# Gate and up projections with 512 moving columns: high and low rows in one matmul, each half in a PSUM bank of its own

## The chip, the cores and the metric

The kernel runs on one core of one Trainium2 chip. The metric is the device time of one execution in microseconds (us). The core has TensorE (PE, with the weight loads shown as PEld), VectorE (DVE), ScalarE (ACT), GpSimd (POOL) and SyncE (SP), which work side by side and wait for one another through semaphores. SBUF is the working memory; PSUM is the memory that TensorE writes into, eight banks of 512 fp32 numbers per partition.

## The reference, cut to what matters

One layer: a mixer (gated MLP beside a gated DeltaNet scan), and then a mixture of 16 experts over 2048 tokens of width 1024. Each expert chooses its 256 tokens, and this part is what the change touches:

```
aff = softmax(h @ w_router + b_router)            # 2048 x 16
gate, idx = top_k(aff of each expert, 256)
xe = h[idx]                                       # 256 x 1024 for each expert
hid = silu(xe @ w_gate[e]) * (xe @ w_up[e])       # 256 x 1024
ye = (hid @ w_down[e]) * gate                     # 256 x 1024
out[idx] += ye
```

All of it is fp32. After the experts comes a last RMSNorm of every token.

## The kernel before, in words

**Products in three parts.** TensorE is given numbers of type fp32r, which keep fewer bits than fp32. So the kernel splits each fp32 operand in two, high (the value cast to fp32r) and low (the value less its high part), and adds three products: high x high, high x low, low x high. `mm3` (L193 to L196) does this for one slice k of 128 of the contraction: L194 is weights high times rows high, L195 weights high times rows low, L196 weights low times rows high, all into the same PSUM columns. A matmul has a stationary operand (128 x 128, loaded ahead of it) and a moving operand, whose columns stream through.

**Loading weights.** `load_w` (L167) brings 512 columns of a weight matrix as two transfers of 256 columns (1 MB each) into `raw`, of which there are two buffers. ACT casts a `raw` into half of the high tile `wh` (L183), DVE subtracts into half of the low tile `wl` (L184). There are three sets of `wh` and `wl`, used in turn (`next_w`). One expert takes six sets, so twelve transfers: gate and up for the first 512 hidden columns, gate and up for the second, and two for down. SyncE issues the transfers in order, each when its buffer is free.

**One expert** (`expert`, L1382). The rows of its tokens come by an indirect gather (`xg`, L1368), are transposed on TensorE into PSUM tiles `xt` (L1376) and split into `xS[0]` (high, by ACT) and `xS[1]` (low, by DVE). The hidden width of 1024 is done in eight pieces f of 128, four for each loaded pair of weights. For each f, one PSUM tile `gu` holds gate in its first 256 columns and up in its second, for the 256 tokens; 8 slices k with 3 matmuls each fill either half, so 48 matmuls of 256 moving columns for one f. Then ACT takes Silu of the gate half (L1396), DVE multiplies with the up half (L1397), ACT casts to the high part of `hS` (L1399) and DVE subtracts for the low part (L1400). The down projection uses `hS` as stationary operand and 512 columns of weights as moving operand, into the tiles `dn`; DVE scales into `ye` (L1416), and POOL adds the rows to `h_rows` by an indirect transfer (L1453). The input of expert e + 1 (`expert_in`: routing with one-hot rows `oh` and matmuls into a tile of pool `c`, then `idx`, gather, transposes) is issued in the middle of expert e. The last three experts add to gathered rows `hr` and write final tokens themselves; during experts 13 and 14 SyncE also loads and stores 16 final tiles of 128 tokens (`final_tile`).

**PSUM in this stage.** Pool `psaD` has three banks for `gu`, `psdD` two for `dn`, `pstD` two for `xt`, and `pscD` one for tile `c`, which serves the top-k search, routing and a few transposes. Eight in all. A `gu` bank comes free when the product (L1397) has read it.

**Order.** Each engine works its own list in order. The lists are made when the kernel is built, by a planner that runs through the program with estimated durations (the tile context is made with `schedule_with_timeline_sim=True`); so matmuls of one expert's down projection stand between those of the next expert's gate and up.

Of the kernel before, what the change touches and what calls it, by code (L numbers as in the profile page):

```python
# [7 lines left out]
F32 = mybir.dt.float32  # L8
F32R = mybir.dt.float32r
# [3 lines left out]
AF = mybir.ActivationFunctionType  # L13
OP = mybir.AluOpType
AX = mybir.AxisListType
PS = bass.MemoryType.PSUM
DR = bass.MemoryType.DRAM

P = 128
D = 1024  # L20
KT = 8
# [1184 lines left out]
def moe(tc, ctx, env):  # L1206
    nc = tc.nc
# [5 lines left out]
    with ExitStack() as pd:  # L1213
# [2 lines left out]
            raw_f = pf.enter_context(tc.tile_pool(name="rawF", bufs=2, side="right"))  # L1216
            pre = [load_w(raw_f, wr, w[0, 0, :, 0:512], nc.gpsimd, parts=PP, cast=C1) for w in (w_gate, w_up)]
        rt = pd.enter_context(tc.tile_pool(name="rtD", bufs=1))
        ps_a = pd.enter_context(tc.tile_pool(name="psaD", bufs=3, space=PS))
        ps_d = pd.enter_context(tc.tile_pool(name="psdD", bufs=2, space=PS))  # L1220
        ps_t = pd.enter_context(tc.tile_pool(name="pstD", bufs=2, space=PS))
        ps_c = pd.enter_context(tc.tile_pool(name="pscD", bufs=1, space=PS))

        tk = ExitStack()
        wk = tk.enter_context(tc.tile_pool(name="wkT", bufs=1))
        vp = ps_c.tile([P, 2, P], F32, name="c")
        for s in range(2):
            nc.tensor.transpose(vp[:, s, :], AFF[:, s].rearrange("p e g -> p (e g)"), ident)
        blkb, belb, cand, step, cK, siob = topc
# [11 lines left out]
        candp = cps[:, 0, 0:60].rearrange("p (i j) -> p i j", j=4)  # L1241
        nc.scalar.activation(candp, cand, AF.Copy)
        for i in range(15):
            tp = ps_c.tile([P, 512], F32, name="c")
            nc.tensor.matmul(tp[:, 0:3], blkb, cK, start=True, stop=False)
            cn = wk.tile([P, 2], BF, name="cn", bufs=15)
            for j in range(2):
                jk = wk.tile([P, 256], BF, name=f"jk{j}", bufs=1)
                cj = nc.vector.tensor_scalar(jk, X, cd[:, j:j + 1], None, op0=OP.is_le, op1=OP.add,
                                             accum_out=cn[:, j:j + 1])  # L1250
            if i == VI:
                after_first = cj
            ca = wk.tile([P, 1], BF, name="ca", bufs=15)
            jk = wk.tile([P, 256], BF, name="jk2", bufs=1)
            with nc.allow_low_precision(reason="whole numbers up to 256 are exact"):
                nc.scalar.activation(jk, X, AF.Sign, scale=-1.0, bias=cd[:, 2:3], accum_out=ca)
            nc.tensor.matmul(tp[:, 0:2], blkb, cn, start=False, stop=False)
            nc.tensor.matmul(tp[:, 2:3], blkb, ca, start=False, stop=True)
            if i not in (6, 14):
                tcd = cps[:, 1, 4 * i:4 * i + 4]  # L1260
                nc.vector.tensor_scalar(tcd, candp[:, i + 1, :], cd[:, 3:4], None, op0=OP.add)
            if i == 14:
                lob = wk.tile([P, 1], F32, name="lob", bufs=1)
                nc.vector.tensor_scalar(lob, cd[:, 3:4], -1.0, float(LO0), op0=OP.mult, op1=OP.add)
            ge = wk.tile([P, 3], F32, name="ge", bufs=15)
            inc = wk.tile([P, 1], F32, name="inc", bufs=15)
            nc.vector.scalar_tensor_tensor(ge, tp[:, 0:3], CAP - 0.5, step[:, i:i + 1].to_broadcast([P, 3]),
                                           op0=OP.is_ge, op1=OP.mult, accum_out=inc)
            if i == 6:
                npre = wk.tile([P, 1], F32, name="npre", bufs=1)  # L1270
                nc.vector.tensor_tensor(npre, cd[:, 3:4], inc, op=OP.subtract)
                t1 = wk.tile([P, 256], U16, name="t1", bufs=1)
                t2 = wk.tile([P, 256], U16, name="t2", bufs=1)
                nc.vector.scalar_tensor_tensor(t1, nhi, npre, nlow, op0=OP.is_equal, op1=OP.mult)
                nc.vector.tensor_scalar(t2, nhi, npre, float(LO0), op0=OP.is_gt, op1=OP.mult)
                nc.vector.tensor_tensor(t1, t1, t2, op=OP.max)
                X = t1
                cd = cand[:, 7, :]
                hb = wk.tile([P, 1], I32, name="hb", bufs=1)
                nc.vector.tensor_scalar(hb, npre, -65536.0, 65536.0 * HI0, op0=OP.mult, op1=OP.add)  # L1280
            elif i < 14:
                cd = wk.tile([P, 4], F32, name="cd", bufs=15)
                nc.vector.tensor_scalar(cd, tcd, inc, None, op0=OP.subtract)
# [7 lines left out]
        eq = wk.tile([P, 256], BF, name="eq", bufs=1)  # L1291
        nc.vector.tensor_scalar(gt, V, thr, None, op0=OP.is_gt, op1=OP.add, accum_out=ct[:, 0:1])
        nc.vector.tensor_scalar(eq, V, thr, None, op0=OP.is_equal, op1=OP.add, accum_out=ct[:, 1:2])
        tp = ps_c.tile([P, 512], F32, name="c")
        nc.tensor.matmul(tp[:, 0:2], belb, ct, start=True, stop=True)
        nc.tensor.matmul(tp[:, 2:3], blkb, ct[:, 0:1], start=True, stop=True)
        off = wk.tile([P, 3], F32, name="off", bufs=1)
# [11 lines left out]
        nc.vector.scalar_tensor_tensor(se, se, off[:, 1:2], eq, op0=OP.add, op1=OP.mult)  # L1309
        nc.vector.scalar_tensor_tensor(sg, sg, BIG, se, op0=OP.add, op1=OP.add)  # L1310
        SL = rt.tile([P, 2, NE, 8], F32, name="SL", bufs=1)
        sp = ps_c.tile([P, 2, P], F32, name="c")
        for s in range(2):
            nc.tensor.transpose(sp[:, s, :], sg[:, s * P:(s + 1) * P], ident)
        nc.vector.tensor_copy(SL.rearrange("p s e g -> p s (e g)"), sp)
# [16 lines left out]
        wk = pd.enter_context(tc.tile_pool(name="wkD", bufs=1))  # L1332

        def route(e):
            oh = ohp.tile([P, 2, 8, 256], BF, name="oh", bufs=1)
            for s in range(2):
                for g in range(8):
                    nc.vector.tensor_scalar(oh[:, s, g, :], siob, SL[:, s, e, g:g + 1], None, op0=OP.is_equal)
            rp = ps_c.tile([P, 2, 256], F32, name="c")
            for hf in range(2):  # L1340
                for i in range(16):
                    s, g = divmod(i, 8)
                    nc.tensor.matmul(rp[:, hf, 0:5], oh[:, s, g, hf * P:(hf + 1) * P], vals[:, s, e, g, :],
                                     start=(i == 0), stop=(i == 15))
            idx = rt.tile([P, 2], I32, name="idx", bufs=2)
            with nc.allow_low_precision(reason="token numbers are whole"):
                nc.vector.tensor_reduce(idx, rp[:, :, 0:2], axis=AX.X, op=OP.add)
            rs = rt.tile([P, 2, 5], F32, name="rs", bufs=2)
            nc.vector.tensor_copy(rs, rp[:, :, 0:5])
            gate = rt.tile([P, 2], F32, name="gate", bufs=2)  # L1350
            nc.vector.tensor_tensor(gate, rs[:, :, 2], rs[:, :, 3], op=OP.add)
            nc.vector.tensor_tensor(gate, gate, rs[:, :, 4], op=OP.add)
            return idx, gate
# [10 lines left out]
        def expert_in(e):  # L1364
            idx, gate = route(e)
            xg = wk.tile([P, 2, D], F32, name="xg", bufs=1)
            for hf in range(2):
                last[1] = nc.gpsimd.indirect_dma_start(out=xg[:, hf, :], out_offset=None, in_=f_rows,  # L1368
                                                       in_offset=bass.IndirectOffsetOnAxis(ap=idx[:, hf:hf + 1], axis=0))
            xS = [wk.tile([P, KT, 256], F32R, name=f"xS{s}", bufs=1) for s in range(2)]  # L1370
            for kk in range(4):
                ps = ps_t.tile([P, 2, 256], F32, name="xt")
                for k2 in range(2):
                    for hf in range(2):
                        k = 2 * kk + k2
                        nc.tensor.transpose(ps[:, k2, hf * P:(hf + 1) * P], xg[:, hf, k * P:(k + 1) * P], ident)  # L1376
                ks = slice(2 * kk, 2 * kk + 2)
                nc.scalar.activation(xS[0][:, ks, :], ps, AF.Copy)
                last[0] = nc.vector.tensor_tensor(xS[1][:, ks, :], ps, xS[0][:, ks, :].bitcast(F32), op=OP.subtract)
            return idx, gate, xS  # L1380

        def expert(e, st, mid=None):  # L1382
            idx, gate, xS = st
            nx = None
            hS = [wk.tile([P, KT, 256], F32R, name=f"hS{s}", bufs=1) for s in range(2)]
            for i in range(2):
                gw = next_w(w_gate[0, e, :, i * 512:(i + 1) * 512])
                uw = next_w(w_up[0, e, :, i * 512:(i + 1) * 512])
                for f in range(4):
                    fs = slice(f * P, (f + 1) * P)  # L1390
                    pg = ps_a.tile([P, 2, 256], F32, name="gu")
                    for j, w in enumerate((gw, uw)):
                        for k in range(KT):
                            mm3(pg[:, j, :], w[0][:, k, fs], w[1][:, k, fs], xS[0][:, k, :], xS[1][:, k, :], k, KT)
                    sg_ = wk.tile([P, 256], F32, name="sgl", bufs=2)
                    nc.scalar.activation(sg_, pg[:, 0, :], AF.Silu)  # L1396
                    nc.vector.tensor_tensor(sg_, sg_, pg[:, 1, :], op=OP.mult)  # L1397
                    ff = 4 * i + f
                    nc.scalar.activation(hS[0][:, ff, :], sg_, AF.Copy)  # L1399
                    nc.vector.tensor_tensor(hS[1][:, ff, :], sg_, hS[0][:, ff, :].bitcast(F32), op=OP.subtract)  # L1400
                if mid is not None and i == 0:
                    nx = mid()
# [192 lines left out]
```

## Time and profile before

| | |
|---|---|
| Time, median of 3 runs (range) | 2490.78 us (2490.44 to 2491.81) |
| Profiled execution: its own time | 2490.03 us |
| Profiled execution: span from first to last instruction | 2488.2 us |
| Mean granted TensorE clock | 0.974 of full speed |
| Busy share of PE, DVE, ACT, POOL | 95%, 64%, 45%, 21% |
| HBM traffic over the span | 211 GB/s |

The page cuts the span into 40 slices and gives each engine's busy share by slice in tenths. A group of instructions (same line, engine, operation and tile) has its busy time, the mean of one in ns, and the idle time of the engine just ahead of it with what ended that. Matmuls are pipelined: one's printed duration overlaps the next one's, so what a matmul costs in a row of them is the time from one start to the next. The chain of waits goes back from the last instruction to what released each step.

### The profile page before, as it was taken

To read this page: it belongs to the slowest core of one execution; us is meant where nothing else is said; L and a number is where in the kernel's file an instruction comes from. 1 tells how busy PE (TensorE), PEld (TensorE's weight loads), DVE (VectorE), ACT (ScalarE), POOL (GpSimd) and SP (SyncE) were. 2 spreads that over 40 slices of the span, in tenths; PEclk is the share of its full clock that TensorE was granted. 3 is DMA by queue.
4 is the path that set the end of the run, shared out by engine and by line. 5 is a ranking of instruction groups with operands and counts; after the bars stand their busy time and mean duration, and the time that the engine had idled before them with its cause. 6 is when DMAs were issued, how large, how long until landed. Compare 5 with 4: busy or idle time off the path is not lost.

```text
span 2488.2 us, 43191 instructions
## 1 busy us (share of the span) xinstructions
PE 2358.8 (95%) x16841; PEld 2156.8 (87%) x16841; DVE 1584.1 (64%) x3339; ACT 1115.6 (45%) x2004; POOL 533.7 (21%) x451
## 2 busy tenths in 40 slices
PE   7999999999997989999949999999999999999998
PEld 4999999887776888888838899999999999998897
DVE  7588765458778646576774556555565565556675
ACT  4554555567633443333332444444444444444453
POOL 2321222211114553232250101101111011011111
PEclk9999999999998999999978999999999999999999
DMA  8676655489956897655563667666676666668884
GB/s 267 199 229 208 208 172 164 134 269 325 284 142 192 253 278 233 197 187 175 174 189 111 203 187 223 199 205 204 203 220 200 207 219 199 210 203 261 305 301 166
DMA packets 473056, 528.97 MB, mean 213 GB/s; under 512 B 104500, under 2 KB 392061, under 8 KB 470803
## 3 DMA queue, kind: packets, MB, share of 16 engines
q1 hardware_dynamic: 455298, 465.63, 58.6%
q0 software_dynamic: 17120, 59.77, 8.3%
q8 instruction: 133, 2.18, 0.4%
q10 hardware_dynamic: 432, 0.79, 0.1%
q14 instruction: 73, 0.59, 0.1%
HBM read 400.45 MB, written 125.67 MB: 211 GB/s over the span
## 4 chain that ended last, share of the span: by engine, by line
PE 45%; DMA 9%; DVE 3%; issue 3%; ACT 1%; POOL 1%; SPq 0%; POOLq 0%; DVEq 0%; ACTq 0%
PE gu L196 7%; PE gu L194 7%; PE gu L195 7%; PE dn L194 4%; PE dn L195 4%; PE dn L196 4%; DMA xg<-f_rows,idx 4%; PE mx L194 2%; PE mx L196 2%; PE mx L195 2%; DMA raw<-in_w_gate_dram 1%; ACT wh L183 1%; PE xt L1376 1%; DVE wl L184 1%; DMA raw<-in_w_up_dram 1%
## 5 line engine op out<-in xcount | busy, mean ns | idle before, releaser
L184 DVE TENSOR_TENSOR wl<-raw,wh 128x2048 fp32r<-128x2048 f32 (+1 forms) x214 | 450.4, 2116 | 294.2 <-ACT wh L183 291.4
L194 PE MATMUL gu<-xS,wh 128*128 128x256 f32 x2048 | 582.8, 286 | 6.6 <-ACT wh L183 4.7
L196 PE MATMUL gu<-xS,wl 128*128 128x256 f32 x2048 | 580.4, 286 | 4.2 <-DVE wl L184 4.2
L195 PE MATMUL gu<-xS,wh 128*128 128x256 f32 x2048 | 582.0, 285 | 0.0
L183 ACT ACTIVATE wh<-raw 128x2048 fp32r<-128x2048 f32 (+1 forms) x218 | 381.8, 1771 | 356.0 <-DMA raw<-in_w_gate_dram 142.7
L194 PEld LDWEIGHTS gu<-xS,wh 128*128 128x128 f32 x2048 | 395.9, 194 | 8.7 <-ACT wh L183 5.3
L196 PEld LDWEIGHTS gu<-xS,wl 128*128 128x128 f32 x2048 | 394.2, 193 | 6.0 <-DVE wl L184 5.0
L195 PEld LDWEIGHTS gu<-xS,wh 128*128 128x128 f32 x2048 | 396.1, 193 | 1.1
L194 PE MATMUL pj<-aS,wh 128*128 128x258 f32 x832 | 238.7, 290 | 3.1 <-DVE y L460 2.7
L195 PE MATMUL pj<-aS,wh 128*128 128x258 f32 x832 | 239.0, 288 | 0.2 <-DVE aS L358 0.2
L196 PE MATMUL pj<-aS,wl 128*128 128x258 f32 x832 | 238.3, 288 | 0.9 <-DVE wl L184 0.9
L1453 POOL DMA_INDIRECT h_rows<-ye,idx x26 | 67.4, 2591 | 659.8 <-DVE ye L1416 565.7
L194 PE MATMUL dn<-wh,hS 128*128 128x512 f32 (+1 forms) x520 | 202.7, 390 | 0.0
L195 PE MATMUL dn<-wl,hS 128*128 128x512 f32 (+1 forms) x520 | 201.2, 387 | 0.0
L196 PE MATMUL dn<-wh,hS 128*128 128x512 f32 (+1 forms) x520 | 200.3, 386 | 0.0
L194 PEld LDWEIGHTS pj<-aS,wh 128*128 128x128 f32 x832 | 157.7, 191 | 4.7 <-issue 2.4
L195 PEld LDWEIGHTS pj<-aS,wh 128*128 128x128 f32 x832 | 159.2, 191 | 0.6 <-DVE aS L358 0.4
L196 PEld LDWEIGHTS pj<-aS,wl 128*128 128x128 f32 x832 | 158.5, 191 | 1.3 <-DVE wl L184 1.1
L194 PE MATMUL uv<-wh,ast 128*128 128x512 f32 x384 | 153.1, 399 | 0.0
L196 PE MATMUL uv<-wh,ast 128*128 128x512 f32 x384 | 150.2, 391 | 0.0
L195 PE MATMUL uv<-wl,ast 128*128 128x512 f32 x384 | 149.8, 390 | 0.0
L1399 ACT ACTIVATE hS<-sgl 128x256 fp32r<-128x256 f32 x128 | 53.1, 415 | 181.9 <-DVE sgl L1397 181.6
(480 smaller groups left out, 4562.7 us busy)
## 6 DMA issues: line engine op xcount, KB each, us to landing
raw<-in_w_gate_dram SPq DMA_DIRECT2D x64, 1024.0 KB
raw<-in_w_up_dram SPq DMA_DIRECT2D x64, 1024.0 KB
raw<-in_w_down_dram SPq DMA_DIRECT2D x64, 1024.0 KB
kv<-kv SPq DMA_DIRECT2D x140, 256.0 KB
raw<-in_w_mod_dram SPq DMA_DIRECT2D x18, 1024.0 KB
a_sp<-aS SPq DMA_DIRECT2D x32, 512.0 KB
ast<-a_sp POOLq DMA_DIRECT2D x16, 1024.0 KB, 8.6
raw<-in_w_in_dram SPq DMA_DIRECT2D x12, 1024.0 KB
```

The lines of the kernel that those rows point to most:

```text
L183: nc.scalar.activation(wh[:, ks, s:s + 256], raw[:, ks], AF.Copy)
L184: (lo_eng or nc.vector).tensor_tensor(wl[:, ks, s:s + 256], raw[:, ks], wh[:, ks, s:s + 256].bitcast(F32), op=OP.subtract)
L194: pace(nc.tensor.matmul(ps, ah, bh, start=(k == 0), stop=False), after)
L195: nc.tensor.matmul(ps, ah, bl, start=False, stop=False)
L196: return nc.tensor.matmul(ps, al, bh, start=False, stop=(k == nk - 1))
L1376: nc.tensor.transpose(ps[:, k2, hf * P:(hf + 1) * P], xg[:, hf, k * P:(k + 1) * P], ident)
L1399: nc.scalar.activation(hS[0][:, ff, :], sg_, AF.Copy)
L1453: nc.gpsimd.indirect_dma_start(out=h_rows, out_offset=bass.IndirectOffsetOnAxis(ap=idx[:, hf:hf + 1], axis=0), in_=ye[:, hf, :], in_offset ...
```

## The change

The two tiles `xS[0]` and `xS[1]` become one tile `xS` with the high and the low rows one after the other. For one k of gate (or up), a single matmul takes weights high as stationary operand and moves both, 256 columns of high rows and 256 of low rows (two stretches of SBUF that lie 8 x 256 numbers apart), into a whole bank: columns 0 to 255 get high x high, 256 to 511 get high x low. A second matmul adds weights low x rows high to the first 256 columns. So gate and up of one f need a bank each; `psaD` has four banks, and `pscD` goes: its tiles now come out of `pstD`, under the name `xt`, in turn with the transposes. When a bank is done, ACT copies its second half to SBUF and DVE adds the first half to it; for gate, ACT then takes Silu in SBUF; when up is done as well, DVE multiplies the two in SBUF.

```diff
-        ps_a = pd.enter_context(tc.tile_pool(name="psaD", bufs=3, space=PS))
+        ps_a = pd.enter_context(tc.tile_pool(name="psaD", bufs=4, space=PS))
         ps_d = pd.enter_context(tc.tile_pool(name="psdD", bufs=2, space=PS))
         ps_t = pd.enter_context(tc.tile_pool(name="pstD", bufs=2, space=PS))
-        ps_c = pd.enter_context(tc.tile_pool(name="pscD", bufs=1, space=PS))
+        ps_c = ps_t
...
-        vp = ps_c.tile([P, 2, P], F32, name="c")
+        vp = ps_c.tile([P, 2, P], F32, name="xt")
...
-            rp = ps_c.tile([P, 2, 256], F32, name="c")
+            rp = ps_c.tile([P, 2, 256], F32, name="xt")
...
-            xS = [wk.tile([P, KT, 256], F32R, name=f"xS{s}", bufs=1) for s in range(2)]
+            xS = wk.tile([P, 2, KT, 256], F32R, name="xS", bufs=1)
...
-                nc.scalar.activation(xS[0][:, ks, :], ps, AF.Copy)
-                last[0] = nc.vector.tensor_tensor(xS[1][:, ks, :], ps, xS[0][:, ks, :].bitcast(F32), op=OP.subtract)
+                nc.scalar.activation(xS[:, 0, ks, :], ps, AF.Copy)
+                last[0] = nc.vector.tensor_tensor(xS[:, 1, ks, :], ps, xS[:, 0, ks, :].bitcast(F32), op=OP.subtract)
...
-                    pg = ps_a.tile([P, 2, 256], F32, name="gu")
+                    gu_ = wk.tile([P, 2, 256], F32, name="gus", bufs=2)
+                    sg_ = gu_[:, 0, :]
                     for j, w in enumerate((gw, uw)):
+                        pg = ps_a.tile([P, 2, 256], F32, name="gu")
                         for k in range(KT):
-                            mm3(pg[:, j, :], w[0][:, k, fs], w[1][:, k, fs], xS[0][:, k, :], xS[1][:, k, :], k, KT)
-                    sg_ = wk.tile([P, 256], F32, name="sgl", bufs=2)
-                    nc.scalar.activation(sg_, pg[:, 0, :], AF.Silu)
-                    nc.vector.tensor_tensor(sg_, sg_, pg[:, 1, :], op=OP.mult)
+                            nc.tensor.matmul(pg, w[0][:, k, fs], xS[:, :, k, :], start=(k == 0), stop=False)
+                            nc.tensor.matmul(pg[:, 0], w[1][:, k, fs], xS[:, 0, k, :], start=False, stop=(k == KT - 1))
+                        nc.scalar.activation(gu_[:, j], pg[:, 1], AF.Copy)
+                        nc.vector.tensor_tensor(gu_[:, j], pg[:, 0], gu_[:, j], op=OP.add)
+                        if j == 0:
+                            nc.scalar.activation(sg_, sg_, AF.Silu)
+                    nc.vector.tensor_tensor(sg_, sg_, gu_[:, 1, :], op=OP.mult)
```

The other tiles of pool `c` (in the top-k search) change their name in the same way.

## Rows read from the trace of the kernel before

**Rows 1.** The page: busy us of each engine (share of the span), instructions.
```profile
PE 2358.8 (95%) x16841; PEld 2156.8 (87%) x16841; DVE 1584.1 (64%) x3339; ACT 1115.6 (45%) x2004; POOL 533.7 (21%) x451
```

**Rows 2.** Stretches: busy us of each engine (instructions), clock, DMA share, GB/s.
```profile
1851.00:1922.00 71.00, 70.98 (x531) 66.82 (x531) 42.23 (x59) 30.42 (x32) 9.09 (x4) 1.00 0.68 208
...
2280.00:2364.00 84.00, 75.26 (x535) 69.72 (x536) 58.11 (x79) 41.22 (x52) 17.03 (x17) 0.96 0.87 300
```

**Rows 3.** Timeline of PE, gate and up, expert 4: start us, duration us, instruction.
```profile
1618.84 0.28 PE L194 MATMUL gu<-xS,wh 128*128 128x256 f32 x1
...
1623.88 0.28 PE L194 MATMUL gu<-xS,wh 128*128 128x256 f32 x1
```

**Rows 4.** Timeline of PE, down projection of expert 3, without a break.
```profile
1609.75 0.39 PE L195 MATMUL dn<-wl,hS 128*128 128x512 f32 x1
...
1613.83 0.39 PE L195 MATMUL dn<-wl,hS 128*128 128x512 f32 x1
```

**Rows 5.** Groups by line, 1300 us to the end: count, busy us, mean ns, idle before.
```profile
L194 PE MATMUL gu<-xS,wh 128*128 128x256 f32 x2048 | 582.8, 286 | 6.6 <-ACT wh L183 4.7 <-DVE sgl L1397 1.9
...
L1400 DVE TENSOR_TENSOR hS<-sgl,hS 128x256 fp32r<-128x256 f32 x128 | 54.3, 424 | 49.3 <-ACT hS L1399 48.9 <-issue 0.5
...
L1397 DVE TENSOR_TENSOR sgl<-sgl,gu 128x256 f32<-128x256 f32 x128 | 53.2, 416 | 82.9 <-ACT sgl L1396 82.7
L1399 ACT ACTIVATE hS<-sgl 128x256 fp32r<-128x256 f32 x128 | 53.1, 415 | 181.9 <-DVE sgl L1397 181.6
...
L1396 ACT ACTIVATE sgl<-gu 128x256 f32<-128x256 f32 x128 | 47.9, 374 | 91.3 <-PE gu L196 91.3
```

**Rows 6.** Timelines of PE, ACT and DVE around the fourth f of expert 4.
```profile
1635.64 0.28 PE L196 MATMUL gu<-xS,wl 128*128 128x256 f32 x1
...
1632.96 3.72 ACT L183 ACTIVATE wh<-raw 128x2048 fp32r<-128x2048 f32 x2 [1.41 <-PE gu L195]
1636.58 0.37 ACT L1396 ACTIVATE sgl<-gu 128x256 f32<-128x256 f32 x1
...
1638.24 2.28 DVE L184 TENSOR_TENSOR wl<-raw,wh 128x2048 fp32r<-128x2048 f32 x1
...
1641.03 0.41 DVE L1397 TENSOR_TENSOR sgl<-sgl,gu 128x256 f32<-128x256 f32 x1
```

**Rows 7.** Timelines of PE, ACT and DVE around the first f of expert 9.
```profile
1973.97 0.40 PE L196 MATMUL gu<-xS,wl 128*128 128x256 f32 x2
...
1977.15 1.92 ACT L183 ACTIVATE wh<-raw 128x2048 fp32r<-128x2048 f32 x1 [4.59 <-DMA raw<-in_w_gate_dram]
...
1981.31 0.41 DVE L1397 TENSOR_TENSOR sgl<-sgl,gu 128x256 f32<-128x256 f32 x1
```

**Rows 8.** Timelines of PE and DVE in expert 1.
```profile
1400.54 0.28 PE L196 MATMUL gu<-xS,wl 128*128 128x256 f32 x1
...
1411.11 0.16 DVE L1347 TENSOR_REDUCE idx<-c 128x2 int32<-128x4 f32 x1 [9.03 <-DMA h_rows<-ye,idx]
...
1414.21 0.38 PE L194 MATMUL gu<-xS,wh 128*128 128x256 f32 x1 [1.88 <-DVE sgl L1397]
```

**Rows 9.** Timeline of SyncE's queue, expert 4: start, us from first to last issue.
```profile
1610.15 3.24 SPq L177 DMA_DIRECT2D raw<-in_w_gate_dram  x2
1619.64 3.79 SPq L177 DMA_DIRECT2D raw<-in_w_up_dram  x2
1637.22 0.37 SPq L177 DMA_DIRECT2D raw<-in_w_down_dram  x1
```

**Rows 10.** Groups by line from 2226 to 2437 us.
```profile
L194 PE MATMUL gu<-xS,wh 128*128 128x256 f32 x342 | 99.1, 290 | 4.7 <-ACT wh L183 4.7
L196 PE MATMUL gu<-xS,wl 128*128 128x256 f32 x342 | 98.6, 289 | 3.5 <-DVE wl L184 3.5
```

**Rows 11.** The chain that ended last, in order of time: start, us, what.
```profile
2324.36 1.93 ACT wh L183
...
2328.63 5.10 DMA raw<-in_w_up_dram
```

More of the change, by code (lines that the diff above doesn't have):

```diff
@@ L1243, in moe @@
         for i in range(15):
-            tp = ps_c.tile([P, 512], F32, name="c")
+            tp = ps_c.tile([P, 512], F32, name="xt")
             nc.tensor.matmul(tp[:, 0:3], blkb, cK, start=True, stop=False)
@@ L1293, in moe @@
         nc.vector.tensor_scalar(eq, V, thr, None, op0=OP.is_equal, op1=OP.add, accum_out=ct[:, 1:2])
-        tp = ps_c.tile([P, 512], F32, name="c")
+        tp = ps_c.tile([P, 512], F32, name="xt")
         nc.tensor.matmul(tp[:, 0:2], belb, ct, start=True, stop=True)
@@ L1311, in moe @@
         SL = rt.tile([P, 2, NE, 8], F32, name="SL", bufs=1)
-        sp = ps_c.tile([P, 2, P], F32, name="c")
+        sp = ps_c.tile([P, 2, P], F32, name="xt")
         for s in range(2):
```

## The prediction

> **What bounds the kernel now.** I read the page's busy shares first, then the stretches, then TensorE's own timeline, and last the waits and the chain. TensorE is busy 95% of the span [rows 1]. Busy time alone can mislead, since matmuls are pipelined, so the reader should look at starts. The change is inside the expert loop, from about 1320 us to the end. In a middle expert PE is busy for all 71.0 us of the stretch at a granted clock of 1.00, DVE for 42 and ACT for 30, the 16 DMA engines 68% [rows 2]: one expert costs 71 us because TensorE needs 71 us. In the last stage but one (2280 to 2364) this is no longer so: PE has 75.3 of 84 us and DMA stands at 87% [rows 2].
>
> Inside gate and up, matmul starts are evenly spaced: 42 starts from the first to the last row shown, 5.04 us, so 120.0 ns per 256-column matmul [rows 3]. In the down projection, with 512 columns, 18 starts take 4.08 us, 226.7 ns each [rows 4]. The durations printed (283 to 390 ns) overlap and are not the price; the spacing is. The difference is 106.7 ns for 256 more columns, which is 2.4 GHz, so each matmul with its weight load carries 13.3 ns that do not depend on its columns.
>
> **What the change removes on TensorE.** For one k of one gate or up group, before: three matmuls of 256 columns, 3 x 120.0 = 360.0 ns. After: one of 512 and one of 256, 226.7 + 120.0 = 346.7 ns. The columns streamed are the same 768; one of three fixed parts goes, 13.3 ns. There are 2048 such k steps (the count of each of the three lines in [rows 5]), so 27.3 us in all, 1.7 us of an expert's 71.
>
> The Trainium skill, "TensorE: Matmul & The Clock Gate", section "Back-to-back issue gap", speaks against this size: it gives an isolated gap of N/2.4 + 2.5 ns. By it the pair of 256-column matmuls would cost 218.4 ns and the 512-column one 215.8, a gain of 2.6 ns a step or 5.3 us in all, where the two spacings above give 27.3. The same section says that weight loads can lift the spacing above that formula; here it is 120.0 against its 109.2. The measured spacing decides.
>
> One thing has no row: the 512 moving columns are two runs of 256 that lie apart in SBUF (high rows, then low rows). Bounds: nothing (226.7 ns, the one-run row), or the fixed part paid once per run (240.0, two 256-column starts), which would leave no gain at all. I take nothing extra, because the row for the same column count is the nearest one, and keep the other end as a rival.
>
> **What part of it reaches the end.** From 2226 to 2437 us the chain of waits runs mostly through the weight chain and the final tiles, not TensorE: raw lands, ACT casts it, DVE subtracts, and the next transfer waits for that [rows 11]. PE waits there for wh and wl, 4.7 and 3.5 us on the two gate/up lines, and 342 of the 2048 steps lie in it [rows 10]. Making PE faster there makes those waits longer. I count these 342 x 13.3 = 4.6 us as lost, and the other 1706 steps as kept: 22.7 us. That the loads keep pace with faster experts before it I read from SyncE: pairs of raw transfers start 9.5 us apart when nothing holds them, 4.75 us each, 57 us for an expert's twelve, and then SyncE pauses 17.6 us before the down weights [rows 9]. So a 69.3 us expert still leaves some 12 us.
>
> **What it adds on ACT and DVE.** Per f, one Silu out of PSUM (374 ns), one product (416), one cast to hS (415) and one subtraction (424) now [rows 5]. Afterwards: two copies out of PSUM on ACT (priced as the Silu, 374 each), two additions on DVE (as the product, 416 each), a Silu from SBUF (as the cast, 415), the product from SBUF (as the subtraction, 424), cast and subtraction as before. ACT goes from 0.79 to 1.58 us per f, DVE from 0.84 to 1.68. For eight f that is +6.3 and +6.7 us per expert, making ACT 37 and DVE 49 of 69 us. Neither becomes the bound; PE's work covers it, where a bank is free.
>
> **Banks.** This is the cover that can fail. Before, a bank holds gate and up of one f and there are three: after an f ends, its bank is needed again two f later, 2 x 48 x 0.12 = 11.5 us. After, each half has its own bank out of four, needed again three halves later: 3 x 8 x 0.3467 = 8.3 us. A bank is held until two operations have passed (Silu and product before, copy and addition after: nearly the same 0.8 us), but their engines are in order. The commonest long hold is at the fourth f of an expert: its last matmul starts at 1635.64 and ends 0.28 later, ACT is in two casts of wh until 1636.58, and DVE's product comes only at 1641.03, behind a subtraction for wl of 2.28 us: 5.5 us to the release at 1641.44 [rows 6]. The longest between experts 2 and 12 that I found: last matmul over at about 1974.3, the cast on ACT first waits 4.59 us for its DMA, product done at 1981.72, some 7.4 us [rows 7]. Both fit under 8.3, the second with 0.9 us to spare and 0.8 us of added ACT work per f in front of it. Cost: none at the common place, at most some 2 us for each of a few long ones, so 0 to 8; I take 1.5.
>
> In expert 1 it already fails: DVE stands 9.03 us at idx, waiting for a scatter to h_rows, and PE stops 1.88 us for a bank [rows 8]. With an 8.3 us window, if both additions of the f whose last matmul started at 1400.54 sit behind idx, PE stops from about 1406.2 to 1414.2, 8.0 us, 6.1 more; if the first one sits ahead, 3.3 more; if both do, the 1.88 goes. I take 3.5.
>
> **Other edits.** The one-bank pool c moves into xt, which rotates over two banks. The top-k search gets two buffers instead of one, but its constant matmul already runs beside DVE's counting: 0, at best a fraction of a us. A route tile now sits between xt tiles; it is released by idx and rs before the gather that the next xt waits for: 0. One xS tile for two changes which address, not who waits: 0; a 512-column matmul needs the low rows too, which the second matmul needed one start earlier. In the last stage the added ACT and DVE work stands beside the weight chain: 2.5 experts x 13 = 33 us. The chain's listing is on ACT or DVE for about a quarter of that stretch, so 8 us if every step met waits for the whole operation, 0 if the additions fall into the waits for raw; I take 2, nearer the low end, since ACT stands idle for raw between the casts. At the end, the last f has one more operation before hS, 0.4 us: 0.5. The order on each engine is set again when the kernel is built, from estimates that I can't see; a few us either way.
>
> **Sum.** The profiled execution took 2490.03 us (span 2488.2). -22.7 +3.5 +1.5 +2 +0.5 = -15.2, so 2474.8; the runs' median is 0.75 us above that execution, so **2475.5**.
>
> **Rivals.**
> - *All of it arrives.* The last stage gains too (PE's waits on the gate and up lines are only 8.2 of its 211 us, so PE was nearly the bound there) and no bank stalls: 2490.8 - 27.3 + 0.5 = 2464. Against: the weight chain above.
> - *The banks run out* in each expert. ACT's copy stands behind a cast that waits for DMA, DVE's addition behind wl, the next Silu on ACT waits for that addition and delays the next cast. If holds at the first and fourth f come to 10.1 us (5.5 plus two more wl of 2.29), PE stops 1.8 us twice in 12 experts: +43 us, 2518. It decides against the change from about 9 us (24 x 0.65 = 15.2). For it: the holds of 5.5 and 7.4. Against: the common one leaves 2.8 us, and PE waited for a bank once in 16 experts.
> - *The two-run operand is paid per run*: 240 + 120 = 360, no gain, and the 7.5 us of costs remain: 2498, slower. It decides from 9 ns per matmul (15.2 of 22.7 us). Nothing in the trace speaks for it. The page's 2.5 ns formula, were it true of removed matmuls, is the milder form: -5.3 + 7.5, 2493.
>
> **Chances.** A change under 0.2% (5 us) can't be told from none. Forecast 0.55 (own range 2467 to 2484), all of it 0.15, banks 0.2 (half of it within 0.2%, a third above), operand 0.1 (two thirds of it above). Faster 0.73, same 0.13, slower 0.14. Range 2461 to 2497: below it a better order than the old one, above it the heavy end of the banks.
>
> **What would show it.** Spacing in gate and up of 0.227 and 0.120, mean 0.173; 2048 fewer matmuls on PE; middle experts of 69 to 69.5 us; two copies and two additions more per f, near 374 and 416 ns; waits of PE for the addition's release of gu, a few us in expert 1 and nearly none in the middle experts; the weight chain from about 2205 on as long as now. The forecast is wrong if the 512-column spacing is over 0.235, or PE's waits for gu exceed 1 us per expert.

## The result, and the profile after

The changed kernel takes 2567.61 us (median of 4 runs, 2560.21 to 2569.24) beside 2491.3 for the kernel before on the same chip: ratio 1.030, 95% interval 1.0281 to 1.0319. It is 3% slower; the forecast was 2475.5 with a range of 2461 to 2497. Its profiled execution took 2566.63 us, span 2564.8, mean granted clock 0.963 (0.974 before). The first gate matmul starts at 1321.21 us (1321.20 before) and TensorE's last ends at 2555.85 (2479.27), so the whole loss of 76.6 us lies between them, in the expert loop.

The page of the kernel after, busy times first, then the four groups of gate and up; these answer to [rows 1, 5].
```profile
PE 2372.4 (92%) x14793; PEld 2057.1 (80%) x14793; DVE 1671.8 (65%) x3595; ACT 1199.9 (47%) x2260; POOL 512.9 (20%) x451
...
L1396 PE MATMUL gu<-xS,wh 128*128 128x512 f32 x2048 | 749.4, 407 | 42.5 <-ACT wh L183 21.3
...
L1397 PE MATMUL gu<-xS,wl 128*128 128x256 f32 x2048 | 585.3, 286 | 9.1 <-DVE wl L184 9.1
...
L1398 ACT ACTIVATE gus<-gu 128x256 f32<-128x256 f32 x256 | 93.3, 376 | 141.4 <-PE gu L1397 138.5
...
L1399 DVE TENSOR_TENSOR gus<-gu,gus 128x256 f32<-128x256 f32 x256 | 103.3, 417 | 60.7 <-ACT gus L1398 59.8
```

2048 matmuls are gone, copy and addition cost 376 and 417 ns where 374 and 416 were predicted. So the pieces have the predicted size. The timeline of PE in gate and up after (compare [rows 3]) shows the spacing too:
```profile
1701.11 0.39 PE L1396 MATMUL gu<-xS,wh 128*128 128x512 f32 x1
1701.34 0.28 PE L1397 MATMUL gu<-xS,wl 128*128 128x256 f32 x1
1701.45 0.39 PE L1396 MATMUL gu<-xS,wh 128*128 128x512 f32 x1
...
1702.49 0.39 PE L1396 MATMUL gu<-xS,wh 128*128 128x512 f32 x1
```
From 1701.11 to 1702.49 stand four pairs, 1.38 us, 0.345 each; 0.3467 was predicted, 0.360 before. The saving is there, and PE still got slower. The stretches say where (compare [rows 2]: 70.98 busy of 71.00, clock 1.00):
```profile
1640.00:1715.00 75.00, 68.94 (x378) 58.13 (x378) 45.30 (x83) 32.28 (x45) 3.72 (x3) 0.95 0.60 185
1715.00:1790.00 75.00, 71.92 (x410) 60.84 (x410) 48.34 (x57) 37.89 (x50) 8.95 (x5) 1.00 0.64 199
```
Two experts, from the end of f7 (the last of the eight f) in expert 3 to that in expert 5, now take 152.4 us, 76.2 each (142.1 and 71.1 before). In the first of the stretches TensorE is idle for 6 us and its granted clock is 0.95. The waits of PE from 1330 us to the end (line, releaser: us in all, times, longest):
```profile
PE gu L1396 <- ACT wh L183: 21.3, 13, 4.4
PE xt L1376 <- DMA xg<-f_rows,idx: 13.6, 13, 1.7
PE gu L1396 <- DVE gus L1399: 10.2, 9, 2.7
PE gu L1397 <- DVE wl L184: 9.1, 7, 3.1
PE gu L1396 <- DVE xS L1379: 7.6, 6, 1.4
```
All of PE's waits there come to 80.9 us, against 16.8 before, so 64.1 more. The clock's deficit over the span, 0.037 x 2564.8 less 0.026 x 2488.2, is at most 30.2 us more. With the 27.3 saved, that gives at most 67.0 of the 76.6; the other 9.6 us, or more, I have not placed. The wait for a bank (`DVE gus L1399`), on which a rival was built, is only 10.2 us.

Where the waits come from is seen at the end of an expert. Below is f7 of expert 4 in the kernel after: PE, then ACT, then DVE, then SyncE's issue of the next expert's gate and up weights.
```profile
1668.57 0.63 PE L194 MATMUL dn<-wh,hS 128*128 128x512 f32 x2
...
1672.89 0.39 PE L1396 MATMUL gu<-xS,wh 128*128 128x512 f32 x1
...
1678.41 0.28 PE L1397 MATMUL gu<-xS,wl 128*128 128x256 f32 x1
...
1697.97 1.22 PE L1396 MATMUL gu<-xS,wh 128*128 128x512 f32 x2 [4.44 <-ACT wh L183]
...
1699.84 0.63 PE L1396 MATMUL gu<-xS,wh 128*128 128x512 f32 x1
...
1700.48 0.63 PE L1396 MATMUL gu<-xS,wh 128*128 128x512 f32 x1
```
```profile
1680.62 0.40 ACT L1398 ACTIVATE gus<-gu 128x256 f32<-128x256 f32 x1
...
1685.32 1.91 ACT L183 ACTIVATE wh<-raw 128x2048 fp32r<-128x2048 f32 x1 [0.31 <-DMA raw<-in_w_gate_dram]
...
1687.61 0.41 ACT L1404 ACTIVATE hS<-gus 128x256 fp32r<-128x256 f32 x1
...
1696.01 1.91 ACT L183 ACTIVATE wh<-raw 128x2048 fp32r<-128x2048 f32 x1 [2.46 <-DMA raw<-in_w_up_dram]
```
```profile
1683.67 0.41 DVE L1399 TENSOR_TENSOR gus<-gu,gus 128x256 f32<-128x256 f32 x1
1684.19 0.42 DVE L1402 TENSOR_TENSOR gus<-gus 128x256 f32<-128x256 f32 x1
...
1687.26 2.29 DVE L184 TENSOR_TENSOR wl<-raw,wh 128x2048 fp32r<-128x2048 f32 x1
...
1691.83 0.42 DVE L1405 TENSOR_TENSOR hS<-gus,hS 128x256 fp32r<-128x256 f32 x1
```
```profile
1680.05 2.57 SPq L177 DMA_DIRECT2D raw<-in_w_gate_dram  x2
1689.58 5.66 SPq L177 DMA_DIRECT2D raw<-in_w_up_dram  x2
```
The same way in the same expert of the kernel before, from f7's last matmul to `hS`, and then the up weights, all engines in order of time:
```profile
1660.70 0.28 PE L196 MATMUL gu<-xS,wl 128*128 128x256 f32 x1
...
1665.58 0.41 DVE L1397 TENSOR_TENSOR sgl<-sgl,gu 128x256 f32<-128x256 f32 x1
1666.03 0.42 ACT L1399 ACTIVATE hS<-sgl 128x256 fp32r<-128x256 f32 x1 [3.04 <-DVE sgl L1397]
1666.47 0.43 DVE L1400 TENSOR_TENSOR hS<-sgl,hS 128x256 fp32r<-128x256 f32 x1 [0.48 <-ACT hS L1399]
...
1676.99 1.92 ACT L183 ACTIVATE wh<-raw 128x2048 fp32r<-128x2048 f32 x1 [3.64 <-DMA raw<-in_w_up_dram]
```
Two things are to be seen. First, 19 down matmuls (1668.57 to 1672.89) now stand on PE ahead of f7's 32 matmuls. This is so in every second expert, 2 to 12 (expert 0 has 12 ahead); in the odd ones, 1 to 11, 41 down matmuls stand behind f7 and none ahead. Second, f7's last matmul ends at 1678.69, and its `hS` is done only at 1692.25: 13.6 us. The copy of up waits behind casts, the addition behind a subtraction for `wl` and `xS`, the cast to `hS` behind a cast of the next gate weights, and the last subtraction behind another `wl`. Before, it was 5.9 us (1660.98 to 1666.90). In the experts with nothing ahead of f7 it is 11.2 to 11.4 us, so long as well. Every down bank needs f7 at its last slice k = 7, and there are two such banks: PE can fill both up to k = 6 (2 x 7 x 3 = 42 matmuls, here 19 ahead of f7 and 23 behind it) and then has nothing of this expert left until `hS` is there and the banks are read. The transfers of the next expert's gate weights start 1.4 us after f7's end as before (1.3), but 4.3 us of the down work that covers the next expert's weights is already spent. The 4.44 us that PE has waited at 1697.97 are for the up weights, which follow the gate weights: their cast on ACT starts 17.3 us after f7's end, only 1.3 us later than before (16.0). After this wait the pairs are 0.64 us apart (1699.84 to 1700.48), which is 768 columns at 1.2 GHz, until 1701.11; the granted clock is 0.50 from 1697.9 to 1701.1 and 1.00 behind it.

### The profile page after: what moved, and what is told of

Same layout as the page of the kernel before. It is cut to its first block, busy times and chain, and to the rows that moved or that the text cites. A ratio compares the mean times of both kernels' runs of the same rounds, so it can differ in the third digit from the quotient of the medians.

```text
span 2564.8 us, 39711 instructions
## 1 busy us (share of the span) xinstructions
PE 2372.4 (92%) x14793; PEld 2057.1 (80%) x14793; DVE 1671.8 (65%) x3595; ACT 1199.9 (47%) x2260; POOL 512.9 (20%) x451
## 5 line engine op out<-in xcount | busy, mean ns | idle before, releaser
L1396 PE MATMUL gu<-xS,wh 128*128 128x512 f32 x2048 | 749.4, 407 | 42.5 <-ACT wh L183 21.3
L1396 PEld LDWEIGHTS gu<-xS,wh 128*128 128x128 f32 x2048 | 395.0, 193 | 141.9 <-ACT wh L183 24.4
L1458 POOL DMA_INDIRECT h_rows<-ye,idx x26 | 55.5, 2133 | 749.9 <-DVE ye L1421 671.9
L1398 ACT ACTIVATE gus<-gu 128x256 f32<-128x256 f32 x256 | 93.3, 376 | 141.4 <-PE gu L1397 138.5
L1399 DVE TENSOR_TENSOR gus<-gu,gus 128x256 f32<-128x256 f32 x256 | 103.3, 417 | 60.7 <-ACT gus L1398 59.8
L194 PEld LDWEIGHTS dn<-wh,hS 128*128 128x128 f32 x520 | 98.3, 190 | 29.7 <-DVE ye L1421 6.5
```

What stands on the lines that cost most here:

```text
L194: pace(nc.tensor.matmul(ps, ah, bh, start=(k == 0), stop=False), after)
L1396: nc.tensor.matmul(pg, w[0][:, k, fs], xS[:, :, k, :], start=(k == 0), stop=False)
L1398: nc.scalar.activation(gu_[:, j], pg[:, 1], AF.Copy)
L1399: nc.vector.tensor_tensor(gu_[:, j], pg[:, 0], gu_[:, j], op=OP.add)
L1458: nc.gpsimd.indirect_dma_start(out=h_rows, out_offset=bass.IndirectOffsetOnAxis(ap=idx[:, hf:hf + 1], axis=0), in_=ye[:, hf, :], in_offset ...
```

## The experiments

Ratios are to the kernel before, run on the same chip; its median on the chips used lay between 2491.3 and 2495.8 us, so differences in us between runs of different experiments are good to a few us.

**e1: the change of pools alone**, on the kernel before.
```diff
-  psaD bufs=3 ... pscD bufs=1
+  psaD bufs=4, ps_c = ps_t
```


> The kernel before with the pool edits alone: four gu banks (each still holding gate and up of one f), pool c merged into xt; matmuls and drains as before. Theory banks (the drain of each half holds the four banks too long): no harm from the pools, 2485 to 2493 us. Theory shared pool (routing tiles in turn with the transposes delay gather, transposes and xS): most of the 76 us is here, 2530 to 2560. Theory work (the added ACT and DVE operations delay the weight casts): 2485 to 2493.


2483.07 us, 0.9964 [0.9941, 0.9987]. Not the cost; a gain of some 9 us that neither theory had. What makes it is open.

**e2: no copies, no additions**; Silu and product read the first half of the bank, so high x low is left out of the result.
```diff
-  nc.scalar.activation(gu_[:, j], pg[:, 1], AF.Copy)
-  nc.vector.tensor_tensor(gu_[:, j], pg[:, 0], gu_[:, j], op=OP.add)
-  nc.scalar.activation(sg_, sg_, AF.Silu)
+  nc.scalar.activation(sg_, pg[:, 0], AF.Silu)
```


> The changed kernel without the two copies and two additions per f: Silu and product read the first half of the bank directly, so high weights x low rows is computed and left out of the result. 512-column matmuls, one half per bank, shared pool stay. Theory banks or work (the added drain operations are the cause): 2460 to 2475, the gain that was forecast. Theory shared pool: stays over 2530. Theory four banks of one half are too few in themselves, whatever the drain: 2500 to 2560.


2470.07 us, 0.9898 [0.9859, 0.9936]. The matmuls and banks of the change give a gain, 22.6 us with e1's in it, and the 2 + 2 drain operations for each f turn it into the loss: 97.5 us.

**e3: more SBUF buffers for the drain**, three for gate and two for up in place of two for both.
```diff
-  gu_ = wk.tile([P, 2, 256], F32, name="gus", bufs=2)
+  sg_ = wk.tile([P, 256], F32, name="gus", bufs=3)
+  up_ = wk.tile([P, 256], F32, name="ups", bufs=2)
```


> The changed kernel with three SBUF buffers for the gate half (and two for up) in place of two buffers that hold both. Theory SBUF buffer (the copy of a bank waits until hS of two f earlier has been split, so the bank waits as well): 2480 to 2520. Theory banks, work or shared pool: within 10 us of the changed kernel's 2567.


2507.52 us, 1.0052 [1.0027, 1.0077]. 60 us come back from one buffer more, with gate and up in tiles of their own. Down no longer stands ahead of f7's matmuls: after f7 come 41 down matmuls in one piece.

**e4: the 512-column matmul as two of 256** into the same two halves, all else as changed.
```diff
-  matmul(pg, w[0][:, k, fs], xS[:, :, k, :], start=(k == 0))
+  matmul(pg[:, 0], w[0][:, k, fs], xS[:, 0, k, :], start=(k == 0))
+  matmul(pg[:, 1], w[0][:, k, fs], xS[:, 1, k, :], start=False)
```


> The changed kernel with its 512-column matmul cut in two of 256 columns (high rows into the first half of the bank, low rows into the second): 2048 more matmuls, everything else as changed. If the merged matmul saves 13.3 ns and its time counts, this is up to 27 us slower than the changed kernel, 2575 to 2595. Theory banks: TensorE is slower and the window of a bank grows from 8.3 to 8.6 us, so it is slower by less, or even not: 2555 to 2580.


2569.62 us, 1.0293 [1.0262, 1.0324], as the changed kernel (1.0281 to 1.0319). In this kernel the merged matmul is worth nothing that can be measured, which fits that TensorE no longer sets the time. It is not a clean test: the list on PE came out another way, with 17 down matmuls ahead of f7 in two experts of three where the changed kernel has 19 in every second. Its PE has no wait for a `gu` bank in the loop, and the time is as long.

**e5: order alone.** The buffers stay two; each down bank's first matmul must stand on PE behind the last gate or up matmul of its expert.
```diff
-  dw[0][...], dw[1][...], k, KT)
+  dw[0][...], dw[1][...], k, KT, after=lastgu if k == 0 else None)
```


> The changed kernel with each group of down matmuls ordered on TensorE behind the last gate/up matmul of its own expert (an order on one engine, no wait is added). The two SBUF buffers stay. Theory order (the list that the planner made spends down matmuls ahead of the last f, and these are then missing as cover while the next expert's first weights come): most of the 60 us goes, 2490 to 2520. Theory hold (the two buffers themselves stop TensorE, whatever the order): PE waits at the last f instead, 2550 to 2580.


2511.44 us, 1.0081 [1.0057, 1.0106]. The order by itself brings 56 us back. In both traces 41 down matmuls stand behind f7 and none ahead, so e3's buffer and e5's order undo the same thing. The longest wait for a bank even rises to 5.9 us:
```profile
PE gu L1396 <- DVE xS L1379: 18.1, 13, 2.1
PE gu L1396 <- DVE gus L1399: 13.7, 11, 5.9
```

**e6 and e7: 512 columns for gate only, and for up only**, each with e3's buffers; the other half by `mm3` as before.
```diff
+  if j != WIDE: mm3(pg[:, 0], ..., k, KT)      # WIDE = 0 (e6), 1 (e7)
```


> The kernel of e3 with the 512-column matmul for gate alone; up is done as before with three matmuls of 256 columns into its own bank and read by the product directly. Half the saved matmuls (1024, 13.6 us) and half the added operations (one copy and one addition per f). Theory SBUF buffer plus work: between the kernel without the drain (2470) and e3 (2507), about 2475 to 2490. If only the merged matmul counted it would be 2478.

> The same for up alone: gate as before with Silu out of PSUM, up with the 512-column matmul, copy and addition. The gate half is held as in e3. Theory work (one addition and one copy per f less than e3): 2475 to 2495. Theory SBUF buffer: near e6, a little worse because the gate half is held while up is copied and added.


2514.0 us, 1.0082 [1.0054, 1.0111], and 2508.46, 1.0059 [1.0037, 1.0082]. Both missed: with half the drain a large part of the loss should have gone, and all of e3's stays. It does not go with the amount of drain work. Why is seen in e6 around f7 of expert 4, whose last matmul ends at about 1659.7: the gate half alone has copy and addition, and the cast to `hS` and its subtraction again stand behind the next gate weights, 11.2 us to the end of `hS`. Behind up's last matmul e6 has the same three operations as the kernel before (product, cast, subtraction), and the product ends 5.3 us after it (5.0 before). So it is not their number that makes the way long: ACT's list puts the cast to `hS` behind a weight cast that waits for its transfer.
```profile
1664.61 0.41 DVE L1407 TENSOR_TENSOR gus<-gus,gu 128x256 f32<-128x256 f32 x1
1668.22 2.29 DVE L184 TENSOR_TENSOR wl<-raw,wh 128x2048 fp32r<-128x2048 f32 x1 [3.20 <-ACT wh L183]
1670.43 0.41 DVE L1410 TENSOR_TENSOR hS<-gus,hS 128x256 fp32r<-128x256 f32 x1
```
```profile
1666.27 1.92 ACT L183 ACTIVATE wh<-raw 128x2048 fp32r<-128x2048 f32 x1 [4.28 <-DMA raw<-in_w_gate_dram]
1668.09 0.40 ACT L1409 ACTIVATE hS<-gus 128x256 fp32r<-128x256 f32 x1
```

**e8: four and two buffers** (two constants of the scan moved out of the way for room).
```diff
-  name="gus", bufs=3
+  name="gus", bufs=4
```


> The kernel of e3 with four SBUF buffers for the gate half instead of three (1 KB found by placing two early constants in the early pool). Theory SBUF buffer still binds at three: 2475 to 2495. Theory work (what is left above the 2470 of the run without the drain is the added ACT and DVE operations in the planner's order): 2500 to 2510, as e3.


2501.86 us, 1.0036 [1.0018, 1.0054]. Little more than e3, so buffers are no longer it. PE now waits at the start of the next expert, for the low rows `xS`, which DVE makes at the same place as f7's drain:
```profile
PE gu L1396 <- DVE xS L1379: 20.4, 13, 2.5
```

**e9 and e10: a strict order**, e8 and the changed kernel with e5's order and also the next expert's gate and up behind the last down matmul.
```diff
+  pace(first gate/up matmul of each bank, lastdn[0])
+  dnm = mm3(..., after=lastgu if k == 0 else None)
```


> The kernel of e8 (four and two SBUF buffers) with both orders set on TensorE: down behind the last gate/up matmul of its expert, and every gate/up group of the next expert behind the last down matmul. Theory order at the boundary (what is left is the next expert's first gate/up matmuls, put ahead of down matmuls while xS is not ready): 2465 to 2485. Theory work (ACT and DVE are too late with what PE needs, in whatever order): 2500 to 2515, with the waits moved to wh, wl or the down banks.

> The changed kernel (two SBUF buffers) with the same two orders. Theory order: some 5 to 10 us above e9, for the waits at the last f that e5 showed (13.7 us of waits for the addition). Theory hold: 2505 or more, as e5.


2528.28 us, 1.0121 [1.0079, 1.0164], and 2525.67, 1.0123 [1.0094, 1.0152]. Slower than e8, and e9 is above both of its ranges: this strict order of PE doesn't hide f7. With nothing of the next expert allowed in between, the wait shows once an expert, for a down bank whose `ye` waits for f7 (the kernel before wasn't run in this order, so how much of the wait is the order's own is open):
```profile
PE dn L194 <- DVE ye L1422: 41.3, 16, 5.1
```
And with the order fixed, the change's buffers (e10) and e8's (e9) cost the same.

**e11: e8, with f7 of every expert as before** (three 256-column matmuls, Silu and product straight from PSUM).
```diff
+  NARROW = ((), (3,))
+  if f in NARROW[i]:
+      for k in range(KT): mm3(pg[:, 0], ..., k, KT)
+      if j == 0: nc.scalar.activation(sg_, pg[:, 0], AF.Silu)
```


> The kernel of e8 (four and two SBUF buffers, no order set) with the last f of each expert as before: three matmuls of 256 columns per k for gate and up, Silu and product straight out of PSUM. The other seven f keep the 512-column matmul. Theory last f (what is left above 2470 is the longer way from the last gate/up matmul to hS: 11 us in e9 where the kernel before had 5.9, and both down banks wait for it): 2470 to 2488, with the one f giving up 3.4 us of the gain. Theory work over all f: 2495 to 2505.


2475.27 us, 0.9916 [0.9884, 0.9948]: 26.6 us less than e8, and faster than before.

**e12: priority**, e8 with the drain operations put into the planner's highest priority.
```diff
+  with tc.high_priority():  # copy, add, Silu; product, cast, subtract
```


> The kernel of e8 with the drains of every f (copy, addition, Silu, product, cast and subtraction) given the highest priority in the planner, so that they go ahead of the weight casts and subtractions that are ready at the same time. Theory last f: the way to hS gets shorter by one or two weight operations (2 to 4 us), 2480 to 2495. If the weight chain is what binds, putting it behind the drains makes it slower: 2505 to 2530.


2501.73 us, 1.0034 [1.0018, 1.0049], as e8. A miss: asking for the drain first did not shorten the way to `hS`. It is 11.2 us in expert 4, where the cast to `hS` (1667.78) still stands behind the weight cast that waits for its transfer (1665.96). So the run doesn't show what the drain would cost with the cast to `hS` first; no run sets the order on ACT or DVE.

**e13: the changed kernel with its two buffers, f7 as before.** The one edit that should undo all of the loss, if f7 is its cause, and little of it, if the buffers are.
```diff
+  NARROW = ((), (3,))      # gu_ with bufs=2 as in the change
```


> The changed kernel with its two SBUF buffers, and only the last f of each expert as before (256-column matmuls, drained straight out of PSUM). Theory two causes (buffers for some 60 us, last f for some 27): 2520 to 2545. Theory one cause (the last f's way to hS, which the buffers only lengthen: the last f waits for the buffer of two f before): 2475 to 2495, as with four buffers.


2480.8 us, 0.9947 [0.9928, 0.9965]: 86.8 us less than the changed kernel, with 7 of 8 f as changed and both buffers as changed. DVE and ACT around the end of f7, whose matmuls end at 1655.54:
```profile
1656.73 0.41 DVE L1411 TENSOR_TENSOR gus<-gus,gu 128x256 f32<-128x256 f32 x1
...
1660.46 0.42 DVE L1414 TENSOR_TENSOR hS<-gus,hS 128x256 fp32r<-128x256 f32 x1
```
```profile
1657.42 0.43 ACT L1413 ACTIVATE hS<-gus 128x256 fp32r<-128x256 f32 x1
1661.93 1.92 ACT L183 ACTIVATE wh<-raw 128x2048 fp32r<-128x2048 f32 x1 [4.08 <-DMA raw<-in_w_gate_dram]
```
`hS` is done at 1660.88, 5.3 us after the matmuls, ahead of the next gate cast on ACT. The down matmuls are back behind f7 (41 in one piece; only expert 0 and one of the last have some ahead), and PE waits 7.5 us for `wl` and 6.2 for `wh` in the whole loop:
```profile
PE gu L1405 <- DVE wl L184: 7.5, 5, 1.9
PE gu L1404 <- ACT wh L183: 6.2, 4, 3.2
```

**e14: the reverse, only f7 changed**, seven f as before (pools and buffers of e8).
```diff
+  NARROW = ((0, 1, 2, 3), (0, 1, 2))
```


> The reverse: four and two buffers, and only the last f of each expert with the 512-column matmul and its longer drain, the other seven as before. Theory last f: the pools' 2483 less 3.4 plus what the last f costs (2502 less 2475, 27 us, and the 3.4 back): 2500 to 2515. Theory total work of ACT and DVE: near the pools' 2483.


2523.11 us, 1.0127 [1.0104, 1.0149]. One f in eight costs 29.8 us against the kernel before and 40.0 against the pools alone (e1), with buffers to spare; that is above both ranges. (The seven other f here have a bank for each half, as changed, so neither kernel is its exact counterpart.) Its DVE and ACT, with f7's matmuls over at 1659.67:
```profile
1665.18 0.43 DVE L1410 TENSOR_TENSOR gus<-gus,ups 128x256 f32<-128x256 f32 x1
1668.15 2.29 DVE L184 TENSOR_TENSOR wl<-raw,wh 128x2048 fp32r<-128x2048 f32 x1 [2.54 <-ACT wh L183]
1670.36 0.42 DVE L1413 TENSOR_TENSOR hS<-gus,hS 128x256 fp32r<-128x256 f32 x1
```
```profile
1666.20 1.92 ACT L183 ACTIVATE wh<-raw 128x2048 fp32r<-128x2048 f32 x1 [3.88 <-DMA raw<-in_w_gate_dram]
1668.03 0.40 ACT L1412 ACTIVATE hS<-gus 128x256 fp32r<-128x256 f32 x1
```
The product ends at 1665.61, 5.94 us after the matmuls, where it was 5.01 before (1660.98 to 1665.99). Those 0.9 us are the price of the extra operations. But now ACT's next item is the cast of the gate weights, and the cast to `hS` follows it: 2.42 us after the product's end, 0.04 before. And the subtraction stands behind the `wl` of these weights: 2.33 us after the start of the cast to `hS`, 0.44 before. 0.9 + 2.4 + 1.9 = 5.2 us, and 11.1 in place of 5.9. Then PE waits at the same place as in e8:
```profile
PE gu L195 <- DVE xS L1379: 19.3, 13, 2.1
```

**e15: the fourth f of either half as before** (f3 too, behind which a weight pair's casts stand in [rows 6]), on e11.
```diff
-  NARROW = ((), (3,))
+  NARROW = ((3,), (3,))
```


> The kernel of e11 with the last f of both halves of the hidden width as before. If the fourth f (whose bank is held longest, 5.5 us before, and whose way nobody waits for) costs nothing, it loses its 3.4 us: 2476 to 2482. If it costs as well: 2465 to 2473.


2468.69 us, 0.9906 [0.9886, 0.9926]. The fastest median of all; its interval and e11's overlap, so what f3 adds beyond f7 isn't settled. What is left of PE's waits on weights:
```profile
PE gu L1403 <- ACT wh L183: 2.6, 1, 2.6
...
PE dn L194 <- ACT wh L183: 1.5, 1, 1.5
```

## Why the prediction was wrong, by its own steps

**The failed step** is this: "At the end, the last f has one more operation before hS, 0.4 us: 0.5." It was counted once, at the end of the kernel, as one operation's length. It stands at the end of each of the 16 experts, and its price is what an engine's list puts ahead of each operation. Shown: e13 takes the change away from f7 alone and the kernel goes from 2567.6 to 2480.8; e14 makes it in f7 alone and pays 29.8 us against the kernel before, 1.9 an expert; e8 against e11 gives 26.6, 1.7 an expert. The way from f7's last matmul to the end of `hS` parts all the kernels: in experts 0 to 3 it is 5.3 to 5.9 us in the kernel before, e1, e2, e11, e13 and e15 (2469 to 2496 us), and 10.9 to 13.5 in all the others (2502 to 2570).

**"A few us either way" for the order** fell too. It was the larger part: with f7's drain in its long form and two buffers, the lists came out with down ahead of f7, and both e5 (order alone) and e3 (one buffer more) give 56 to 60 us back. That the planner turned the list because its own estimates put f7's `hS` too late to wait for is my reading of this; the runs show that the order is the cost, and that a short f7 or a third buffer each prevents it, not why the planner chose it. The same holds for the lists of ACT and DVE, where 4.3 of the 5.2 us that e14's way grew by are order: that a wide f7 brings this order is shown, why is not.

**"PE's work covers it, where a bank is free"** held for seven f of eight: e13 has their 2 + 2 operations and is faster than before. It failed where PE's work ends. The page's sums (DVE 65%, ACT 47%) can't show this, and the forecast took them for cover.

**Banks.** The rival of banks had a kindred chain (copy behind cast, addition behind `wl`) but the wrong victim: PE's waits for a bank were 10.2 us in all, twice the 5 (1.5 + 3.5) of the sum, and e5 has more of them and is 56 us faster. The stall that was forecast for expert 1 didn't come; 6.0 of the 10.2 us lie in the last experts, from 2336 us on. With 2518 its price would still have been 50 us short.

**What was right.** The spacing was right, 0.345 for a pair. The operand in two runs costs nothing extra, so that rival is gone. The Trainium skill, "TensorE: Matmul & The Clock Gate", section "Back-to-back issue gap", has 2.5 ns beside the columns in the gap of an isolated matmul. The pair here is 320 ns of columns at 2.4 GHz and 25 ns beside, 12.5 each, so the measurement decides again. The prices of copy and addition were right too. So was the gain where nothing stands in its way: -22.7 was forecast for it, e2 shows -22.6; but e1's 9.6 us, which I gave 0, seem to be part of that, so some 13 would remain for the matmuls, and this agreement is partly luck. A middle expert takes 69.5 us in e2 and 69.7 in e13, where 69.3 was forecast and 71.1 measured before.

Two slips of the prediction bear on nothing here: 24 x 0.65 is 15.6 and not 15.2, and SyncE's pause in [rows 9] is 13.8 us from its last issue, 17.6 from the first of that pair.

Its own marks tell it: "nearly none in the middle experts" for the waits for a bank about held (4.1 us in all up to expert 12), while the 69-us expert didn't come. The wait that appears there, for `wh` once the cover is spent, wasn't among those I had named for a middle expert.

## What to carry to other kernels

Work added to an engine with time to spare is free only as long as something else covers it: look for the place where the covering work runs out, usually the last piece before a dependent phase, and work out that chain step by step with the long operations that each engine's list may put ahead of it. Then give that piece the shortest drain, even if it costs the main engine more; here one f in eight done the old way turned +3.0% into -0.5%, and with more buffers into -0.8%. Where lists are made from estimates, a longer chain may also re-order the main engine, and an order alone cost 56 us here.

## What the runs showed that I had not expected

The wait of 4.44 us on TensorE is followed by matmul pairs at 0.64 us in place of 0.345 until about 3 us later, so this wait costs more than its length. The merged one-bank pool with a fourth `gu` bank made the kernel before 0.36% faster, with runs from 2476.66 to 2495.54; I have no cause for it. And the drain's amount hardly counted: e6 and e7, with half of it, were no faster than e3, and e13, with seven eighths of it, is faster than the kernel before.
